# Start the first products before the shift is known, and take the RMS factors with tokens on partitions

## The chip, the cores and the metric

The kernel runs on one core of a Trainium2 chip. The metric is the device time of one execution in microseconds (us). The kernel before was run three times: median 1080.2 us, from 1079.94 to 1081.06 us. A profile of one more execution lies beside it.

Names of the engines as the profile has them: PE is TensorE (matrix products; PEld is its loading of stationary operands), DVE is VectorE, ACT is ScalarE, POOL is GpSimd, SP is SyncE, which here issues the DMAs.

## The reference, cut to what matters

Two layers of a decoder run over 512 prompt tokens and 8 sample tokens, which are kept side by side as 520 columns. Every layer begins with an RMSNorm whose result is scaled and shifted by vectors that depend on a conditioning input c (adaLN), followed by a wide projection:

```python
def rmsnorm(x, g):
    return x * lax.rsqrt(jnp.mean(x * x, axis=-1, keepdims=True) + EPS) * g
def adaln(c, w, b):
    return jnp.split((jax.nn.silu(c) @ w + b)[:, None, :], 3, axis=-1)
# even layer
shift, scale, gate = adaln(c, aw, ab)
h = rmsnorm(x, g) * (1 + scale) + shift
z = h @ w_in                      # 1024 -> 8192 features
# ... short convolution and dilated window attention on slices of z ...
x = x + gate * (out @ w_out)
# odd layer: the same wrapper, with pooling and retention;
# o of each retention head is normalised over its 256 features:
o = o * lax.rsqrt(jnp.mean(o * o, axis=-1, keepdims=True) + EPS)
```

All data are fp32, and the model width is 1024.

## The kernel before, in words

**Layout.** Features lie on the 128 partitions, tokens in the free dimension: x is eight tiles `xT[j]` of 128 x 520 (512 prompt tokens and 8 samples). An fp32 product is made of three matrix passes on operands split into a high and a low part: high data by high weight, low data by high weight, high data by low weight (`mm3`). One k step of a product (one 128-feature slice) is therefore six MATMULs, each over 256 or 264 columns; a product of eight k steps gives 128 output features for all tokens. There are 144 such weight tiles. ACT makes the high part of a weight (`w_hi`, 128 x 1024), DVE the low part (`w_lo`, two halves of 128 x 512). Lines L135 to L160 are helpers that issue the operations, so most groups of the profile carry L140 (ACT), L146, L149, L153, L154 (DVE) or L160 (PE), and a group is known by its tiles.

**Order of the work.** PE runs the products one after the other without a break. A scheduler (L181 to L215) counts one tick per k step, some 0.72 us. `at(n, f)` runs f n ticks later; `put` and `put_fill` queue attention work that is let in one piece a tick. Each engine executes its instructions in program order, so an early row that waits holds up all rows behind it on that engine. The data loads are all issued by SP.

**The beginning (L384 to L447).** x is loaded, ACT squares the tiles and DVE adds them. Four products with `on_d`, a 128 x 128 tile of 1/1024, sum over the partitions and leave the mean square of each token repeated on every partition. ACT takes the root, DVE the reciprocal (L413, L414: `r0`, 128 x 520), and POOL multiplies the eight tiles by it (L416). Then a loop over j takes the adaLN weight of one feature tile, shift and scale together (`ada_load`, `ada_mm`: eight products with 256 columns), transposes it (`ada_fin`, L348), and makes `h = x * r0 * A + S` (`h_hi`, `h_lo`). Two steps behind, k step j of the first two products runs. Head pair 0 takes its v and k from these two products and its gate and q from the next two.

**The head pairs (`head_pair`, L457 to L616).** Eight head pairs follow. Each makes four products (v, k, gate, q), then causal scores in four blocks, a softmax on DVE and ACT, transposes of the probabilities (`turn`, L543) and the sums over v (`weigh`), all let in between the k steps of the next head pair's products. DVE also works on the samples' window attention (`L573` and the 128 x 1024 products).

**The seam (L796 to L894).** The output products of layer 0 give the new x, tile by tile. A running sum of squares is multiplied by `on_d` (`ssq_add`), the root goes to ACT, two reciprocals to DVE (`r1_part`, L202 by the scheduler) and eight multiplications to POOL (`h1_scale`, L868); `h1_x` and a split then make layer 1's h. The first products of layer 1 run on x scaled but not yet normalised, and their results are multiplied by r1 (`z_first`).

**Retention (`ret_head`, L904 to L1132).** For each of four heads `norm` (L974 to L984) multiplies the head's squares by `on_d` (one product with 512 columns), takes the root on ACT (128 x 512), and DVE takes the reciprocal in two halves (`inv`, L986 to L990) ahead of `gate` (L992).

## Time and profile before

| what | value |
|---|---|
| median of three runs | 1080.2 us |
| profiled execution | 1080.08 us |
| its span | 1078.3 us |
| mean granted TensorE clock | 0.991 of full speed |
| PE busy | 1042.2 us (97%) |
| DVE busy | 638.1 us (59%) |
| ACT busy | 492.3 us (46%) |
| POOL busy | 27.4 us (3%) |

The span is the time from the first to the last instruction on the core; the profiled execution's own time is 1.8 us more. A busy time is the sum over an engine's instructions. A group's row gives the line, the engine, the operation, output and input tiles with their shapes, the count, the busy time and the mean of one in ns, then the time the engine was idle ahead of it and what ended it. A row of a timeline gives the start, the duration, the engine and the operation, and in brackets a wait ahead of it. A row of windows gives a stretch of time, its length, the busy time of PE, PEld, DVE, ACT and POOL with counts, the granted clock of PE as a share, and what the DMA did.

### The profile page before, as it was taken

The numbers are of one execution on the slowest core, as the hardware profiler recorded it, in microseconds if no ns is written. First come the engines' busy times: TensorE is split into PE (matmuls) and PEld (weight loads), VectorE is DVE, ScalarE is ACT, GpSimd is POOL, SyncE is SP. The second block draws the span as 40 slices with busy tenths as digits, with TensorE's granted clock in tenths as the row PEclk, the third lists the DMA queues.
The fourth block names the chain that finished last, engine by engine and source line by source line (L and its number), as shares of the span: only waits on it lengthen the run. The fifth ranks groups of instructions, "written<-read, shape, count | busy, mean of one in ns | idle before, by whom it ended". The sixth has DMA issues, their size and how long they took to land.

```text
span 1078.3 us, 21052 instructions
## 1 busy us (share of the span) xinstructions
PE 1042.2 (97%) x8656; PEld 989.0 (92%) x8656; DVE 638.1 (59%) x1468; ACT 492.3 (46%) x890; POOL 27.4 (3%) x45
## 2 busy tenths in 40 slices
PE   3999999999999999999999989999999999999996
PEld 1699999999989999999999989999999999999996
DVE  6556777667786444446344586565647666674443
ACT  4575667656663222223333465435454444333333
POOL 3000000000000000000000040000000000000000
PEclk9999999999999999999999999999999999999999
DMA  9486545665436355352744335272635423225212
GB/s 356 159 271 189 166 143 161 209 185 181 141 129 195 119 198 159 117 170 91 248 160 150 105 118 195 91 253 98 235 123 178 171 96 109 83 81 181 99 70 80
DMA packets 82177, 168.96 MB, mean 157 GB/s; under 512 B 7209, under 2 KB 47241, under 8 KB 79001
## 3 DMA queue, kind: packets, MB, share of 16 engines
q1 hardware_dynamic: 82080, 167.61, 46.6%
q8 instruction: 68, 1.11, 0.4%
q14 instruction: 29, 0.23, 0.1%
HBM read 149.40 MB, written 18.65 MB: 156 GB/s over the span
## 4 chain that ended last, share of the span: by engine, by line
PE 92%; DVE 4%; ACT 2%; DMA 1%; issue 1%; SPq 0%; DVEq 0%; ACTq 0%
PE mm L160 75%; PE aux L160 13%; PE aux L543 2%; DVE t L146 1%; ACT t L140 1%; DVE wlo L146 1%; DMA v<-vdr 1%; PE aux L348 0%; PE aux L1239 0%; DVE t L149 0%; DMA t<-in_x_t 0%; PE aux L463 0%; DVE t L202 0%; PE aux L918 0%; ACT whi L140 0%
## 5 line engine op out<-in xcount | busy, mean ns | idle before, releaser
L160 PE MATMUL mm<-t,whi 128*128 128x256 f32 (+1 forms) x4608 | 764.5, 287 | 7.1 <-ACT t L140 4.9
L160 PEld LDWEIGHTS mm<-t,whi 128*128 128x128 f32 x4608 | 637.3, 189 | 36.2 <-issue 21.9
L160 PE MATMUL mm<-t,wlo 128*128 128x256 f32 (+2 forms) x2304 | 465.7, 282 | 0.0
L160 PEld LDWEIGHTS mm<-t,wlo 128*128 128x128 f32 x2304 | 358.8, 189 | 0.0
L146 DVE TENSOR_TENSOR wlo<-wraw,whi 128x512 fp32r<-128x512 f32 x288 | 192.6, 699 | 52.0 <-ACT whi L140 51.7
L140 ACT ACTIVATE whi<-wraw 128x1024 fp32r<-128x1024 f32 x144 | 151.6, 1053 | 98.1 <-PE mm L160 62.9
L146 DVE TENSOR_TENSOR t<-t,t 128x520 fp32r<-128x520 f32 (+6 forms) x164 | 107.0, 652 | 96.3 <-ACT t L140 94.6
L140 ACT ACTIVATE t<-t 128x520 fp32r<-128x520 f32 (+3 forms) x116 | 70.9, 616 | 166.0 <-DVE t L149 97.8
L140 ACT ACTIVATE t<-aux 128x128 f32<-128x128 f32 (+7 forms) x148 | 67.9, 469 | 115.9 <-PE aux L160 64.8
L140 ACT ACTIVATE t<-mm 128x512 f32<-128x512 f32 (+2 forms) x116 | 56.4, 507 | 114.0 <-PE mm L160 112.5
L146 DVE TENSOR_TENSOR t<-aux,t 128x512 fp32r<-128x512 f32 (+6 forms) x120 | 60.8, 512 | 37.1 <-ACT t L140 32.0
L160 PE MATMUL aux<-t,t 64*128 64x256 f32 (+6 forms) x384 | 56.2, 329 | 0.0
L160 PE MATMUL aux<-t,v 128*128 128x512 f32 (+2 forms) x224 | 49.1, 324 | 0.6 <-DVE t L146 0.6
L521 DVE CUSTOM_DVE_ANT_0 t<-aux,t 128x128 f32<-128x128 f32 (+3 forms) x64 | 28.9, 489 | 31.9 <-PE aux L160 31.4
L160 PEld LDWEIGHTS aux<-t,t 64*128 64x128 f32 (+1 forms) x384 | 41.5, 186 | 5.4
L140 ACT ACT_TABLE_LOAD x32 | 41.1, 1283 | 1.3 <-PEq L1353 0.7
L140 ACT ACTIVATE t<-t,mn 128x128 f32<-128x128 f32 (+3 forms) x64 | 35.4, 554 | 13.3 <-DVE mn L521 13.1
L160 PEld LDWEIGHTS aux<-t,v 128*128 128x128 f32 x224 | 34.4, 188 | 1.9 <-DVE t L146 0.8
L149 DVE SCALAR_TENSOR_TENSOR big<-v,ksc,big 128x256 f32<-128x256 f32 x64 | 27.7, 480 | 10.3 <-ACT big L140 9.9
L350 DVE TENSOR_REDUCE m<-aux 128x18 f32<-128x72 f32 x24 | 5.5, 231 | 45.8 <-PE aux L348 45.8
L143 DVE COPY zs<-mm 128x8 f32<-128x8 f32 x76 | 12.1, 159 | 34.6 <-ACT t L140 33.7
L146 DVE TENSOR_TENSOR t<-mm,t 128x512 f32<-128x512 f32 (+1 forms) x24 | 16.5, 689 | 26.6 <-PE mm L160 17.4
(145 smaller groups left out, 603.2 us busy)
## 6 DMA issues: line engine op xcount, KB each, us to landing
wraw<-in_w_in_e SPq DMA_DIRECT2D x64, 512.0 KB, 6.4
wraw<-in_w_in_o SPq DMA_DIRECT2D x48, 512.0 KB, 3.2
big<-in_ada_e SPq DMA_DIRECT2D x12, 1024.0 KB, 8.3
big<-in_ada_o SPq DMA_DIRECT2D x12, 1024.0 KB, 8.5
wraw<-in_w_out_e SPq DMA_DIRECT2D x16, 512.0 KB, 3.5
big<-in_state_ret SPq DMA_DIRECT2D x16, 512.0 KB, 7.5
out_new_ret_sample<-big SPq DMA_DIRECT2D x16, 512.0 KB, 3.7
wraw<-in_w_out_o SPq DMA_DIRECT2D x16, 512.0 KB, 3.2
```

The source lines that it names most:

```text
L140: return nc.scalar.activation(out=out, in_=in_, func=func, scale=scale, **kw)
L143: return nc.vector.tensor_copy(out, in_)
L146: return nc.vector.tensor_tensor(out=out, in0=in0, in1=in1, op=op)
L149: return nc.vector.scalar_tensor_tensor(out=out, in0=in0, scalar=scalar, in1=in1, op0=op0, op1=op1)
L160: nc.tensor.matmul(out, lhsT=lhsT, rhs=rhs, start=start, stop=stop)
L350: nc.vector.tensor_reduce(out=m, in_=pt.rearrange("p s (g r) -> p s r g", g=4)[:, :, 0:9, :], op=ALU.add, axis=AX.X)
L521: nc.vector.tensor_tensor_reduce(out=sb, in0=s[:, 0:n], in1=bt[e][:, S - n:S], scale=1.0, scalar=3e38, op0=ALU.add, op1=ALU.min, accum_out=mn,
L543: nc.tensor.transpose(ep[:, c * P:(c + 1) * P], src, ident)
```

## The change

**At the beginning.** The adaLN weight is stored in another order, scale, shift and gate apart, two feature tiles to a load. The identity and the small vectors are loaded earlier. The sum of squares is taken with tokens on partitions: `rms_sums` uses a 128-token block of the squares as the stationary operand and one column of `on_d` as the moving one, so that five one-column products give a 128 x 5 tile; `rms_roots` takes its root and reciprocal, and `rms_rows` turns it into rows again by four products with the identity (128 columns each) and one of 8 columns, which ACT and DVE copy out. `x_normed` multiplies x by it on DVE instead of POOL. The first four products (v, k, gate and q of head pair 0) run on x scaled, without the shift; the first two in four rounds of two k steps, with the scale of the next two tiles made between. The shift's four adaLN groups are made inside products 3 and 4. What the shift adds to the four results is a vector per output: `shift_rows` multiplies the shift by the raw weight of each product (eight products of 128 columns, a transpose, a reduction), and `z_shift` adds it. Head pair 0's pieces come 8 ticks later (`D0`). Head pair 1 runs on x scaled too, with ten further columns that carry the shift (`z_second`). Meanwhile `h_x` and `h_split` make the full h, which head pair 2 and later use.

**At the seam.** `rms_sums`, `rms_roots` and `rms_rows` replace `ssq_add` and `r1_part`; the eight multiplications (`h1_scale`) go from POOL to DVE, one every two ticks.

**In retention.** The same three functions replace the product with 512 columns, the 128 x 512 root and the two 128 x 256 reciprocals of each head; the rows come two ticks behind the sums, and the gates at ticks 5 and 8 instead of 7 and 10.

The diff, cut to its core:

```diff
+    def rows_mm(lhs, raw):
+        n = raw.shape[2] * raw.shape[3]
+        ps = aux([P, n])
+        for k in range(KT):
+            g = 32 * (k % 4)
+            mm(ps[g:g + 32], lhs[:, k, :], raw[:, k].rearrange("p s c -> p (s c)"), k < 4, k >= 4)
...
+    def rms_sums(parts, n=T):
+        blocks = [c * P for c in range(n // P)] + ([n - P] if n % P else [])
+        pc = aux([P, len(blocks)])
+        for i, c in enumerate(blocks):
+            for k, sq in enumerate(parts):
+                mm(pc[:, i:i + 1], sq[:, c:c + P], on_d[:, 0:1], k == 0, k == len(parts) - 1)
+        return pc
+    def rms_roots(pc, scale=1.0):
+        rc = mk(cp, [P, 5], F32, "rc", 2)[:, 0:pc.shape[1]]
+        act(rc, pc, ACTF.Sqrt, bias=eps[:, 0:1], scale=scale)
+        nc.vector.reciprocal(rc, rc)
+        return rc
+    def rms_rows(rc, r):
+        pr, n = aux([P, S]), r.shape[1]
+        for i in range(4):
+            mm(pr[:, i * P:(i + 1) * P], rc[:, i:i + 1].to_broadcast([P, P]), ident, True, True)
+        act(r[:, 0:S], pr)
+        if n > S:
+            pr = aux([P, n - S])
+            mm(pr, rc[:, 4:5].to_broadcast([P, P]), ident[:, P - n + S:P], True, True)
+            vcopy(r[:, S:n], pr)
...
-    for x in xT:
-        nc.gpsimd.tensor_tensor(out=x, in0=x, in1=r0, op=ALU.mult)
...
+    rms_rows(rms_roots(rms_sums([sqa])), r0)
+    def x_normed(j):
+        vtt(xT[j], xT[j], r0, ALU.mult)
+    def x_scaled(j):
+        x, g = xT[j], mA[0][:, j, 8:9]
+        hi, lo = tr(T + 10), tr(T + 10)
+        vtt(xhs[:, j, :], x[:, S:T], mA[0][:, j, 0:NB], ALU.mult)
+        act(hi[:, 0:S], x[:, 0:S], ACTF.Copy, scale=g)
+        act(hi[:, S:T], xhs[:, j, :])
+        stt(lo[:, 0:S], x[:, 0:S], g, f(hi[:, 0:S]), ALU.mult, ALU.subtract)
+        lo_of(lo[:, S:T], xhs[:, j, :], hi[:, S:T])
+        xa.append((hi, lo))
...
+    for i in range(4):
+        for j in (2 * i, 2 * i + 1):
+            x_scaled(j)
...
+        if i < 3:
+            x_normed(2 * i + 2)
+            x_normed(2 * i + 3)
+            if i:
+                first_two(2 * i)
+            md = ada_mm(rawA[i + 1])
+            first_two(2 * i + 1 if i else 0)
+            ada_fin(0, "scale", i + 1, md)
+            if i == 0:
+                first_two(1)
+        else:
+            first_two(6)
+            first_two(7)
...
+    def z_shift(n, md):
+        m, x = zf[n]
+        ws = rows_turn(md)
+        act(x, x, ACTF.Silu if n == 2 else ACTF.Identity, bias=ws[:, 0, 8:9])
+        vtt(zs[0][:, m, :], zs[0][:, m, :], ws[:, 0, 0:NB], ALU.add)
+    for n in range(4):
+        at(1 + 2 * n, shift_rows, n)
...
+    for j in range(KT):
+        at(8 + 2 * j, h_x, j)
+        at(25 + j, h_split, j)
...
-            put(score, qb, after=Q0 + n)
+            put(score, qb, after=D0 + Q0 + n)
...
-    def h1_scale():
-        for x in xT:
-            nc.gpsimd.tensor_tensor(out=x, in0=x, in1=r1, op=ALU.mult)
+    def h1_scale(j):
+        vtt(xT[j], xT[j], r1, ALU.mult)
...
-    at(3, ssq_add, sq, False)
-    at(4, r1_part, 0)
-    at(4, r1_part, 1)
-    at(6, h1_scale)
+    at(2, r1_sums)
     for j in range(KT):
+        at(H1A - 2 + H1B * j, h1_scale, j)
         at(H1A + H1B * j, h1_x, j)
...
         def norm():
-            ms = aux([P, S])
-            mm(ms, on_d, st["sq"][0], True, True)
-            rr = tt(S)
-            act(rr, ms, ACTF.Sqrt, bias=eps[:, 0:1], scale=4.0)
+            rc = rms_roots(rms_sums(st["sq"][0:1], S), 4.0)
...
-            at(1, inv, 0)
-            at(4, inv, 1)
+            at(2, rms_rows, rc, st["rr"])
             for i in range(2):
-                at(7 + 3 * i, gate, i)
+                at(5 + 3 * i, gate, i)
```

How this moves the instructions is seen in three places. The first is PE at the start of the program. In the rows of before, `t_137` and `t_157` are the squares, `big` the adaLN weight, `mm_180` the first product.

```order
L160 MATMUL aux_159<-t_137,on_d 128x256
L160 MATMUL aux_160<-t_137,on_d 128x264
L160 MATMUL aux_159<-t_157,on_d 128x256
L160 MATMUL aux_160<-t_157,on_d 128x264
L160 MATMUL aux_182<-big_125,scT 32x256 x8
L348 MATMUL aux_195<-csm,md_191 128x128 x2
L160 MATMUL aux_207<-big_129,scT 32x256 x8
L348 MATMUL aux_226<-csm,md_216 128x128 x2
L160 MATMUL aux_240<-big_133,scT 32x256 x8
L160 MATMUL mm_180<-t_222,whi_193 128x256
```

The same place after; `rc_171` is the 128 x 5 tile, `csm` holds the identity.

```order
L160 MATMUL aux_165<-on_d,t_140 128x1 x5
L160 MATMUL aux_174<-csm,rc_171 128x128 x4
L160 MATMUL aux_180<-csm,rc_171 128x8
L160 MATMUL aux_185<-big_126,scT 32x256 x8
L354 MATMUL aux_198<-csm,md_194 128x128 x2
L160 MATMUL aux_233<-big_130,scT 32x256 x8
L160 MATMUL mm_183<-t_205,whi_219 128x256
```

The first product stands behind two adaLN groups instead of three, and the rows of r0 stand ahead of the first group.

The second place is ACT around head pair 0's last softmax block and its first transposed probabilities. In the rows of before, `t_763`, `t_765`, `t_827` and `t_829` are probabilities, `t_848` and `v_850` the turned v, `t_898` the first transposed block of probabilities, `wraw` a weight.

```order
L140 ACTIVATE whi_813<-wraw_661 128x1024
L140 ACTIVATE t_763<-t_763,ls_732 128x256
L140 ACTIVATE t_765<-t_765,ls_736 128x256
L140 ACTIVATE t_827,ls_732<-t_827,mn_731 128x512
L140 ACTIVATE t_829,ls_736<-t_829,mn_735 128x512
L140 ACTIVATE t_848<-aux_843 128x512
L140 ACTIVATE v_850<-t_848 128x8x64
L140 ACTIVATE t_827<-t_827,ls_732 128x512
L140 ACTIVATE t_829<-t_829,ls_736 128x512
L140 ACTIVATE t_898<-aux_893 128x512
```

After, the probabilities are `t_934`, `t_936`, `t_1006` and `t_1008`; rows with `mS_88,mA_86` are `h_x`, and `t_205<-t_109` is the first `h_split`.

```order
L140 ACTIVATE t_114<-t_114,mS_88,mA_86 128x512
L140 ACTIVATE t_934<-t_934,ls_891 128x256
L140 ACTIVATE t_936<-t_936,ls_895 128x256
L140 ACTIVATE t_1020<-t_969 128x512
L140 ACTIVATE t_1006,ls_891<-t_1006,mn_890 128x512
L140 ACTIVATE t_1008,ls_895<-t_1008,mn_894 128x512
L140 ACTIVATE t_115<-t_115,mS_88,mA_86 128x512
L140 ACTIVATE t_1006<-t_1006,ls_891 128x512
L140 ACTIVATE t_1008<-t_1008,ls_895 128x512
L140 ACTIVATE t_116<-t_116,mS_88,mA_86 128x512
L140 ACTIVATE t_1074<-aux_1069 128x512
L140 ACT_TABLE_LOAD
```

The rebuilding of h stands between the exponentials and the scalings, and the first transposed block (`t_1074`) stands behind both.

The third place is DVE at the seam. Before, `t_7394` is r1 and the last line's product the first one that layer 1 evicts.

```order
L146 TENSOR_TENSOR t_7373<-mS_89,t_7372 128x10
L146 TENSOR_TENSOR wlo_7429<-wraw_7153,whi_7413 128x512 x2
L202 RECIPROCAL t_7394<-t_7394 128x256
L202 RECIPROCAL t_7394<-t_7394 128x264
L149 SCALAR_TENSOR_TENSOR t_7470<-mm_7400,t_7394 128x512
```

After, r1 is `t_7524`.

```order
L146 TENSOR_TENSOR t_7503<-mS_89,t_7502 128x10
L395 RECIPROCAL rc_7562<-rc_7562 128x5
L146 TENSOR_TENSOR wlo_7571<-wraw_7287,whi_7543 128x512
L143 COPY t_7524<-aux_7579 128x8
L146 TENSOR_TENSOR wlo_7571<-wraw_7287,whi_7543 128x512
L149 SCALAR_TENSOR_TENSOR t_7609<-mm_7530,t_7524 128x512
L143 COPY ws_7610<-mm_7530 128x9
L146 TENSOR_TENSOR zs_95<-mm_7530,t_7524 128x8
L146 TENSOR_TENSOR zs_95<-zs_95,ws_7610 128x8
L146 TENSOR_TENSOR t_6328<-t_6328,t_7524 128x520
```

The two long reciprocals are replaced by one of 128 x 5, and the multiplications by r1 join DVE's queue.

## The prediction

> **What bounds the kernel now.** I read the page first, then the waits of PE, then windows and timelines of the three places that the change touches.

> ```profile
> span 1078.3 us, 21052 instructions
> PE 1042.2 (97%) x8656; PEld 989.0 (92%) x8656; DVE 638.1 (59%) x1468; ACT 492.3 (46%) x890; POOL 27.4 (3%) x45
> ```

> PE is busy for 97% of the span: what the change can give lies in the beginning and in PE's few waits, and a matrix pass added anywhere else is paid in full. The waits (engine, place, what was waited for: us in total, times, longest):

> ```profile
> PE aux L160 <- DVE t L146: 12.7, 4, 10.7
> PE mm L160 <- ACT t L140: 4.9, 2, 4.4
> PE aux L911 <- ACT t L140: 3.7, 1, 3.7
> PE aux L918 <- ACT t L140: 1.3, 2, 1.0
> ```

> 10.7 of the first row is the start, up to the first sum of squares; the second row holds the first product's wait for its data; L911 and L918 are the seam. The stretches (length, busy of PE, PEld, DVE, ACT, POOL, then the granted clock):

> ```profile
> 20.00:25.00 5.00, 1.07 (x16) 0.50 (x16) 4.96 (x6) 0.81 (x1) 5.00 (x5) 0.71 1.01 415
> 25.00:30.00 5.00, 2.74 (x11) 2.44 (x12) 4.96 (x6) 2.67 (x4) 4.45 (x4) 0.50 0.35 146
> 76.00:82.00 6.00, 6.00 (x54) 6.00 (x53) 5.01 (x12) 5.55 (x12) 0.00 (x0) 1.00 0.51 154
> 82.00:88.00 6.00, 6.00 (x59) 5.24 (x58) 6.00 (x9) 3.45 (x8) 0.00 (x0) 1.00 0.06 24
> 625.00:630.00 5.00, 3.39 (x28) 3.17 (x26) 4.36 (x6) 1.73 (x3) 5.00 (x5) 1.00 0.32 108
> 634.00:636.00 2.00, 2.00 (x11) 2.00 (x11) 1.75 (x5) 1.97 (x4) 0.00 (x0) 0.50 0.00 0
> ```

> At 20 to 30 us PE is half idle or more while DVE and POOL are full, and its clock is halved. At 76 to 88, head pair 0's softmax, PE has no gap, but ACT, then DVE, has hardly a moment free: this is where the change puts more work on both. The last two rows are the seam: a wait, and half the clock behind it.

> **The beginning.** Rows of the timeline of before, DVE then PE (start, us, operation):

> ```profile
> 6.66 3.92 DVE L146 TENSOR_TENSOR t<-t,t 128x520 f32<-128x520 f32 x5 [0.41 <-ACT t L140]
> 10.72 3.81 PE L160 MATMUL aux<-t,on_d 128*128 128x256 f32 x8 [10.72 <-DVE t L146]
> 14.46 1.44 PE L160 MATMUL aux<-big,scT 128*32 128x256 f32 x16
> 28.06 0.80 PE L160 MATMUL mm<-t,whi 128*128 128x256 f32 x2 [1.56 <-DVE t L146]
> 63.60 0.63 PE L160 MATMUL mm<-t,whi 128*128 128x256 f32 x4
> 84.75 1.07 PE L160 MATMUL aux<-big,scT 128*32 128x256 f32 x16
> 85.75 0.51 PE L160 MATMUL mm<-t,whi 128*128 128x256 f32 x2
> ```

> Product 1 gets going at 28.06, product 5 (the first of head pair 1) starts at 63.60. An adaLN group of 256 columns costs PE 85.75 − 84.75 = 1.00.

> What small products cost is read where they stand inside a product. Here four calls with 4 columns (two passes each), and elsewhere one with 512, are let in:

> ```profile
> 396.88 0.40 PE L160 MATMUL mm<-t,wlo 128*128 128x256 f32 x2
> 397.12 0.95 PE L160 MATMUL aux<-csm,t 128*128 128x4 f32 x8
> 397.93 0.73 PE L160 MATMUL mm<-t,whi 128*128 128x256 f32 x4
> 398.50 0.40 PE L160 MATMUL mm<-t,wlo 128*128 128x256 f32 x2
> ...
> 399.22 0.40 PE L160 MATMUL mm<-t,wlo 128*128 128x256 f32 x2
> ...
> 682.95 0.40 PE L160 MATMUL mm<-t,wlo 128*128 128x256 f32 x2
> 683.18 1.02 PE L160 MATMUL aux<-t,on_d 128*128 128x512 f32 x2
> ...
> 684.52 0.40 PE L160 MATMUL mm<-t,wlo 128*128 128x256 f32 x2
> ```

> Undisturbed, one wlo row follows the other in 399.22 − 398.50 = 0.72, a k step; eight make a product, 5.75. With the small calls between it is 1.62, with the large one 1.57: 0.90 for four small calls, 0.225 each, and 0.85 for 512 columns, so 0.21 for a call of 128.

> The new chain. DVE's six sums end at 10.58; the seventh, now needed too, makes 11.3. Five one-column calls at half clock 2.2, root, reciprocal of 128 x 5 and their handing over 0.8, five row calls at half clock 2.1: r0 is there at about 16.4. The adaLN group (1.44 as above) ends at 17.5 or a little later; its copy, transposes, reduction and two scales take some 2.0, and then ACT has two scaled tiles and a weight ahead of the first product: 0.8 + 0.8 + 1.0. So it starts at about 22.0. From there to product 5 PE has 8 x 1.44 (two products), 3 x 1.25 (scale groups with transposes), 11.5 (products 3 and 4) and 4 x 1.25 (shift groups), 31.75 in all. It waits besides: after the transposes of the second and third round stands only the product that needs them, and reduction, scales, ACT's scaled tile and DVE's part of it take 2.2; in the first round one product step of 1.44 covers most of that. With 2.2 + 2.2 + 0.8, product 5 starts at 59.0: **−4.6**. The bounds are −6.5 (a start at 21.0 and chains of 1.7) and −2.5 (1.7 lost to half the clock, as at 20 to 30 us, and 0.4 more for the sums).

> POOL's leaving is in this already. The same DVE operations took, at 17.6 to 29.2 us (POOL busy) and at 30 to 47 us (POOL idle):

> ```profile
> L146 DVE TENSOR_TENSOR wlo<-wraw,whi 128x512 fp32r<-128x512 f32 x3 | 4.2, 1411 | 0.0
> L154 DVE TENSOR_SCALAR mA<-m,bsc,pv 128x9 f32<-128x9 f32 x2 | 2.7, 1327 | 0.0
> ```

> ```profile
> L146 DVE TENSOR_TENSOR wlo<-wraw,whi 128x512 fp32r<-128x512 f32 x3 | 2.0, 680 | 0.0
> ...
> L154 DVE TENSOR_SCALAR mA<-m,bsc,pv 128x9 f32<-128x9 f32 x5 | 1.4, 285 | 0.0
> ```

> I use the lower values, since POOL is idle there. [...]

> **What the shift costs PE later.** Four groups of shift rows: eight calls of 128 columns each. From 1.00 at 256 columns, half is 0.50; I take 0.58 because of the price of small calls (ends 0.50 and 1.00). Four: 2.3. Four transposes at 0.12: 0.5. Ten more columns on four products: 0.4. The turn of head pair 0's v, which stood before 63.60, now stands behind: 0.4. Together **+3.6**, with no wait beside it to hide in.

> **Head pair 1's products: a queue on ACT, then on DVE.** Rows for the durations, then one of DVE's window work, then PE's first transpose of head pair 0's probabilities:

> ```profile
> L140 ACT ACTIVATE t<-t,mS,mA 128x512 f32<-128x512 f32 x8 | 6.5, 808 | 3.0 <-DVE mA L154 3.0
> L140 ACT ACT_TABLE_LOAD x32 | 41.1, 1283 | 1.3 <-PEq L1353 0.7
> L140 ACT ACTIVATE whi<-wraw 128x1024 fp32r<-128x1024 f32 x144 | 151.6, 1053 | 98.1 <-PE mm L160 62.9
> L146 DVE TENSOR_TENSOR t<-t,t 128x520 fp32r<-128x520 f32 x64 | 44.7, 698 | 33.1 <-ACT t L140 32.9
> ```

> ```profile
> 81.52 1.21 DVE L573 TENSOR_REDUCE t<-big 128x16 f32<-128x1024 f32 x1
> ```

> ```profile
> 79.09 0.60 PE L543 MATMUL aux<-csm,t 128*128 128x128 f32 x4
> ```

> Before, the first transpose came 79.09 − 63.60 = 15.5 after product 5's start. Now it stands 8 ticks later (5.7), behind the shift rows with their transposes (2.8) and v's turn (0.4): 24.4. ACT's rows from there to the scaling that this transpose reads stand in a fixed order: two table loads 2.6, seven rebuilt tiles at 0.71 (neighbouring rows overlap by 0.1) 5.0, three weights 2.9, and by the same rule from their mean durations eight exponentials 4.2, four scalings 1.7, and 8.4 for evictions, biases, splits and small rows: 24.8. At two places ACT must wait for a product's end or a maximum, 1.9 at least; then one scaling more. So the scaling is ready at some 27.4 and PE waits 3.0.

> Behind it DVE. From the first rebuilt tile's low part to the last one's it has 8 of these (0.6 each), six low parts of transposed blocks, a window product, two reductions (1.1 each) and two halves of a weight, 12.6 in all; PE's nine ticks, six turns and an adaLN group come to 10.1. Before, DVE was already full there (82 to 88) and PE did not wait. Transposes that DVE has not read hold PSUM buffers, and PE waits for those. The excess is 2.5; its bounds are 0 (buffers take it) and 4.8 (all eight low parts are extra). Together **+5.5**, bounds 0 and 9.5, the latter with half the clock behind a longer gap (1.7, as at the seam).

> [...]

> **The seam.**

> ```profile
> 632.06 0.66 PE L911 MATMUL aux<-csm,t 128*128 128x128 f32 x4 [3.67 <-ACT t L140]
> ```

> ```profile
> L868 POOL TENSOR_TENSOR t<-t,t 128x520 f32<-128x520 f32 x8 | 12.1, 1548 | 17.7 <-DVE t L202 17.7
> L202 DVE RECIPROCAL t<-t 128x256 f32<-128x256 f32 x1 | 1.7, 1746 | 0.0
> ```

> PE gets ten one-column calls (2.25) and five of rows (1.1) and is rid of two sums of 520 columns (0.87 each): +1.6. It waits about 0.45 for the last square. The 3.67 goes, since two reciprocals (3.4) leave DVE's queue ahead of the evicted v and their neighbours are no longer slowed by POOL; so does the half clock behind it (3.4 us at half speed, 1.7), and L918's 1.3 falls to about 0.7. DVE gets eight multiplications of 0.6, one in two ticks, which fit. Together 1.6 + 0.45 − 3.67 − 1.7 − 0.6 = **−3.9**; bounds −5.5 and 0 (the multiplications take the place of the reciprocals, and PE waits nearly as before).

> **Retention.** Per head +0.90 (four small calls) +0.87 (rows) −0.85 (512 columns) = 0.92; four heads **+3.7**. What ACT and DVE save there buys nothing: no wait of PE in that part stands in the list above. Bounds 2.0 and 4.5.

> **The sum** against the profiled execution's 1080.08 (span 1078.3; the median, 1080.2, lies 0.1 above it): −4.6 + 3.6 + 5.5 − 3.9 + 3.7 = +4.3, **1084.4 us**. A difference of 0.2%, 2.2 us, is about what a measurement of this kernel can tell from none.

> **The rivals.** *No queue.* ACT and DVE catch up before PE needs them. For it: before, PE did not wait at 76 to 88. Against it: 24.8 us of ACT rows in a fixed order. Sum −1.2: 1078.9.

> *No queue, and a beginning at its best.* PE starts at 21.0 and the chains of the rounds take 1.2 instead of 2.2: −7.6 in place of −4.6, sum −4.2, 1075.9. For it: DVE without POOL's company is idle for much of each round. Against it: the chain crosses three engines, and nothing stands behind it on PE that could go first. This is the other side; it decides from the point where head pair 0's scaling is done before PE has run 24.4 us past product 5's start.

> *A long queue.* All eight low parts count and a gap passes the length that halved the clock: 3.0 + 4.8 + 1.7 in place of 5.5, sum +8.3, 1088.4. For it: DVE's 6.00 of 6.00 at 82 to 88. Against it: at 76 to 82 PE ran on although ACT was busy for 5.55 of 6.

> **How the numbers follow.** Forecast 0.46, no queue 0.20, no queue with the best beginning 0.24, long queue 0.10. Faster takes the third and 0.04 of the second; same takes 0.16 of the second and 0.04 of the forecast's low end; slower the rest: 0.28, 0.20, 0.52. The range goes from 0.9 below the third case (the seam's better bound) to 1.1 above the fourth: 1075.0 to 1089.5. The forecast's own range is 1082 to 1087.

> **What would show it.** Product 5 near 59.0; a wait of PE near 83 for ACT's scaling, and waits of PE on DVE's low parts just behind; no 3.67 wait at the seam and a full clock there; a k step with four one-column calls 0.9 longer. It is wrong if PE runs through head pair 1 without a wait, or if a wait of the beginning stays that I have taken as gone.

## The result, and the profile after

The change makes the kernel slower: 1100.42 us (median of four runs, 1099.19 to 1101.0) against 1080.18 us, a ratio of 1.0183 with a 95% interval of 1.017 to 1.0196. The forecast was 1084.4 us in a range of 1075.0 to 1089.5: the direction was right, the size a fifth of what came.

The profiled execution of the changed kernel took 1101.0 us. Its page and the waits of PE:

```profile
span 1099.2 us, 21418 instructions
PE 1059.0 (96%) x8814; PEld 1007.5 (92%) x8814; DVE 625.9 (57%) x1518; ACT 503.7 (46%) x928; POOL 4.2 (0%) x31
```

```profile
PE aux L160 <- DVE t L146: 18.0, 7, 12.9
PE mm L160 <- ACT t L140: 2.8, 2, 1.4
PE mm L160 <- ACT whi L140: 2.5, 1, 2.5
PE aux L669 <- ACT t L140: 2.2, 1, 2.2
PE aux L1065 <- ACT t L140: 2.1, 2, 1.1
PE aux L160 <- issue: 1.3, 1, 1.3
```

The seam's wait of 3.7 (L911 before) is gone from the list, as forecast. New are L669, the transposes of head pair 0's probabilities waiting for ACT, and five more us in the first row. But the listed waits grow far less than the span does (20.9 us): PE's busy time is 16.8 us higher. A busy PE can be a PE at half clock (4.00 of 4.00 us busy at a clock of 0.50 from 632 to 636 us, below), so I read from the starts of the products where the time came in. A product has 48 MATMULs on `mm` tiles; counting them in PE's timeline gives the start of each (us):

| start of product | before | after | later by | in this stretch |
|---|---|---|---|---|
| 1 | 25.70 | 24.19 | −1.50 | |
| 5 (head pair 1) | 63.60 | 64.84 | 1.24 | beginning: +1.24 |
| 13 (head pair 3) | 130.43 | 146.04 | 15.61 | head pairs 1 and 2: +14.37 |
| 81 (first of layer 1) | 610.67 | 626.72 | 16.05 | +0.44 |
| 89 (first of the second retention head) | 680.79 | 698.05 | 17.25 | seam: +1.20 |
| start of the last MATMUL | 1068.59 | 1089.50 | 20.91 | retention and the rest: +3.66 |

One of the two old sums of the seam, 0.9, stood ahead of product 81 (at 601.16 us before), so that part of the seam's change lies in the row above it: taken whole, the seam lost some 0.3. Product 5 also varies with the execution: in the four other profiles below whose start is that of the kernel before and not filled, it begins between 63.54 and 65.30, and in the four others whose start is that of the change (in one with wider sums), between 64.94 and 65.57. The loss at the beginning is therefore about 1 us, and the gain that was forecast is not there.

The windows of the changed kernel, with the granted clock as the third number from the end, show half a clock in four places: twice in the beginning (from 26.18 and 43.24 us, for 3.41 each), behind the wait of head pair 1 (from 94.44, for 3.41), and at the seam.

```profile
24.00:28.00 4.00, 3.59 (x19) 3.19 (x20) 3.83 (x7) 1.36 (x3) 0.00 (x0) 0.77 0.88 367
40.00:44.00 4.00, 2.31 (x14) 1.86 (x14) 2.76 (x10) 1.65 (x4) 0.00 (x0) 0.91 0.92 341
44.00:48.00 4.00, 3.87 (x22) 3.67 (x21) 0.17 (x1) 1.13 (x3) 0.00 (x0) 0.67 0.12 48
92.00:96.00 4.00, 1.82 (x11) 1.58 (x9) 2.30 (x6) 4.00 (x9) 0.00 (x0) 0.81 0.99 363
96.00:100.00 4.00, 4.00 (x28) 4.00 (x28) 1.27 (x3) 3.97 (x6) 0.00 (x0) 0.77 0.90 250
104.00:108.00 4.00, 2.63 (x18) 2.34 (x17) 4.00 (x7) 1.83 (x4) 0.00 (x0) 1.00 0.25 57
628.00:632.00 4.00, 3.80 (x27) 3.71 (x27) 1.29 (x5) 3.19 (x6) 0.00 (x0) 0.79 0.21 78
632.00:636.00 4.00, 4.00 (x21) 4.00 (x20) 0.28 (x1) 0.21 (x1) 0.00 (x0) 0.50 0.00 0
```

The last row is the one to learn from: PE is busy for 4.00 of 4.00 us, nobody waits, and it has 21 MATMULs at a clock of 0.50, where `seam_only` (below) has 36 in the same place at 1.00. The record of the granted clock has the seam's half clock from 630.34 us for 6.83 us.

PE's timeline of the changed kernel at the places that the prediction named:

```profile
12.91 2.27 PE L160 MATMUL aux<-on_d,t 128*128 128x1 f32 x10 [12.91 <-DVE t L146]
24.19 0.75 PE L160 MATMUL mm<-t,whi 128*128 128x256 f32 x4 [2.54 <-ACT whi L140]
42.22 0.51 PE L160 MATMUL mm<-t,whi 128*128 128x256 f32 x2 [1.40 <-ACT t L140]
43.01 0.62 PE L160 MATMUL mm<-t,whi 128*128 128x256 f32 x2 [0.28 <-DVE t L149]
67.06 0.64 PE L160 MATMUL aux<-v,t 128*32 128x128 f32 x16 [1.32 <-issue]
94.59 0.48 PE L669 MATMUL aux<-csm,t 128*128 128x128 f32 x1 [2.18 <-ACT t L140]
104.89 0.69 PE L160 MATMUL aux<-t,v 128*128 128x512 f32 x2 [0.85 <-DVE t L146]
109.41 0.39 PE L160 MATMUL aux<-t,v 128*128 128x256 f32 x1 [1.92 <-DVE t L146]
628.67 2.51 PE L160 MATMUL aux<-on_d,t 128*128 128x1 f32 x18 [0.20 <-ACT t L140]
```

And ACT just ahead of 94.59, in its order: a tile of h is rebuilt (`t<-t,mS,mA`) between the exponentials and the scaling for which PE waits.

```profile
92.42 0.71 ACT L140 ACTIVATE t<-t,mn 128x512 f32<-128x512 f32 x1
93.03 0.19 ACT L140 ACTIVATION_READ_ACCUMULATOR t<-t,mn 128x1 f32 x1
93.12 0.80 ACT L140 ACTIVATE t<-t,mS,mA 128x512 f32<-128x512 f32 x1
93.83 1.32 ACT L140 ACTIVATE t<-t,ls 128x512 f32<-128x512 f32 x2
```

### The profile page after: what moved, and what is told of

Its sections match the earlier page's. It is cut to its first block, busy times and chain, and to the rows that moved or that the text cites. A ratio compares the mean times of both kernels' runs of the same rounds, so it can differ in the third digit from the quotient of the medians.

```text
span 1099.2 us, 21418 instructions
## 1 busy us (share of the span) xinstructions
PE 1059.0 (96%) x8814; PEld 1007.5 (92%) x8814; DVE 625.9 (57%) x1518; ACT 503.7 (46%) x928; POOL 4.2 (0%) x31
## 4 chain that ended last, share of the span: by engine, by line
PE 88%; ACT 4%; DVE 4%; DMA 1%; issue 1%; SPq 0%; DVEq 0%; ACTq 0%
PE mm L160 72%; PE aux L160 14%; ACT t L140 3%; DVE t L146 2%; PE aux L669 1%; DMA v<-vdr 1%; ACT whi L140 1%; DVE t L149 1%; PE aux L354 1%; DVE wlo L146 0%; DMA t<-in_x_t 0%; PE aux L1377 0%; SPq L157 0%; ACT L140 0%; DVE t L699 0%
## 5 line engine op out<-in xcount | busy, mean ns | idle before, releaser
L160 PE MATMUL mm<-t,whi 128*128 128x256 f32 (+2 forms) x4608 | 766.5, 288 | 6.0 <-ACT t L140 2.8
L160 PEld LDWEIGHTS mm<-t,whi 128*128 128x128 f32 x4608 | 639.1, 190 | 33.5 <-issue 21.4
L160 PE MATMUL mm<-t,wlo 128*128 128x256 f32 (+2 forms) x2304 | 468.7, 284 | 0.2 <-DVE wlo L146 0.2
L160 PEld LDWEIGHTS mm<-t,wlo 128*128 128x128 f32 x2304 | 360.9, 189 | 0.6 <-DVE wlo L146 0.6
L146 DVE TENSOR_TENSOR wlo<-wraw,whi 128x512 fp32r<-128x512 f32 x280 | 182.9, 685 | 43.5 <-ACT whi L140 43.1
L140 ACT ACTIVATE whi<-wraw 128x1024 fp32r<-128x1024 f32 x140 | 147.4, 1053 | 98.1 <-PE mm L160 63.6
L146 DVE TENSOR_TENSOR t<-t,t 128x520 fp32r<-128x520 f32 (+7 forms) x189 | 119.1, 636 | 99.3 <-ACT t L140 97.6
L140 ACT ACTIVATE t<-t 128x520 fp32r<-128x520 f32 (+4 forms) x126 | 73.8, 591 | 156.3 <-DVE t L149 96.0
L140 ACT ACTIVATE t<-aux 128x512 f32<-128x512 f32 (+7 forms) x154 | 71.4, 473 | 119.7 <-PE aux L160 74.2
L140 ACT ACTIVATE t<-mm 128x512 f32<-128x512 f32 (+2 forms) x112 | 54.0, 504 | 108.1 <-PE mm L160 103.9
L146 DVE TENSOR_TENSOR t<-aux,t 128x512 fp32r<-128x512 f32 (+6 forms) x120 | 61.0, 514 | 36.6 <-ACT t L140 31.5
L160 PE MATMUL aux<-t,t 64*128 64x256 f32 (+6 forms) x384 | 56.6, 329 | 0.3 <-DVE t L146 0.3
L160 PE MATMUL aux<-t,v 128*128 128x512 f32 (+2 forms) x224 | 49.5, 325 | 3.4 <-DVE t L146 3.4
L160 PEld LDWEIGHTS aux<-t,t 64*128 64x128 f32 (+1 forms) x384 | 41.8, 186 | 6.1 <-DVE t L146 0.6
L140 ACT ACT_TABLE_LOAD x32 | 41.1, 1283 | 1.3 <-PEq L1489 0.7
L140 ACT ACTIVATE t<-t,mn 128x128 f32<-128x128 f32 (+3 forms) x64 | 35.4, 554 | 11.8 <-DVE mn L647 11.5
L160 PEld LDWEIGHTS aux<-t,v 128*128 128x128 f32 x224 | 34.5, 188 | 5.1 <-DVE t L146 3.0
L356 DVE TENSOR_REDUCE m<-aux 128x18 f32<-128x72 f32 (+1 forms) x28 | 6.4, 227 | 47.8 <-PE aux L354 47.8
L143 DVE COPY zs<-mm 128x8 f32<-128x8 f32 x72 | 11.7, 162 | 38.1 <-ACT t L140 32.9
L146 DVE TENSOR_TENSOR t<-mm,t 128x512 f32<-128x512 f32 (+1 forms) x24 | 16.6, 690 | 26.7 <-PE mm L160 17.8
```

The lines of the kernel that those rows point to most:

```text
L140: return nc.scalar.activation(out=out, in_=in_, func=func, scale=scale, **kw)
L143: return nc.vector.tensor_copy(out, in_)
L146: return nc.vector.tensor_tensor(out=out, in0=in0, in1=in1, op=op)
L160: nc.tensor.matmul(out, lhsT=lhsT, rhs=rhs, start=start, stop=stop)
L356: nc.vector.tensor_reduce(out=m, in_=pt.rearrange("p s (g r) -> p s r g", g=4)[:, :, 0:9, :], op=ALU.add, axis=AX.X)
```

## The experiments

**One part at a time.** The first question is whether the parts add, or hinder one another.

`seam_only` is the kernel before with the seam of the change:

```diff
-    at(3, ssq_add, sq, False)
-    at(4, r1_part, 0)
-    at(4, r1_part, 1)
-    at(6, h1_scale)
+    at(2, r1_sums)
     for j in range(KT):
+        at(H1A - 2 + H1B * j, h1_scale, j)
         at(H1A + H1B * j, h1_x, j)
```

> The kernel before with the seam of the change alone. Theory A (each part costs what the two traces show at its place): the products behind the seam start 1.2 us later than before, 1081.4 us, with the clock halved for some 6.8 us between the sums and the first products of layer 1, and no 3.67 us wait. Theory B (the seam by itself gains what was forecast, and what was lost there came from the state in which the new beginning left the queues): about 3.9 us faster, 1076.3 us, with the clock not halved.

Measured: 1078.57 us against 1080.77, ratio 0.998 (0.9971 to 0.9989). Neither theory: the seam alone is 2.2 us faster. In its profile the products behind the seam (product 89) stand 2.79 us earlier relative to product 5 than before, and its clock is full where the changed kernel had half:

```profile
612.00:616.00 4.00, 3.81 (x34) 3.72 (x33) 1.54 (x4) 2.89 (x6) 0.00 (x0) 1.00 0.18 70
616.00:620.00 4.00, 4.00 (x36) 4.00 (x35) 0.77 (x2) 0.60 (x1) 0.00 (x0) 1.00 0.23 68
```

So the same instructions gained in one kernel and lost in the other, and the clock is what differs. All profiles with the new seam bear this out. From product 81 to 89, the kernel before takes 70.12 us; the new seam takes 68.19 to 68.28 in the six profiles with a full clock there, 69.79 in the one with half a clock for 3.41 us, and 71.33 and 71.34 in the two with half a clock for 6.83.

`ret_only` is the kernel before with the change's retention norm (`rms_sums`, `rms_roots`, `rms_rows` and the gates two ticks earlier).

> The kernel before with the change's retention norm alone. Theory A (small calls on a full engine are paid in full): four times 0.9 us more, 1083.7 us, and each head's products 0.9 us later. Rival (the calls hide in gaps between passes, and the shorter reciprocals let something start earlier): within 0.5 us of before, 1080.2 us.

Measured: 1084.48 us against 1080.77, +3.7, ratio 1.0036 (1.0023 to 1.0049); the last product ends 3.75 us later. The price per call was read rightly. In its timeline one wlo row follows the next by 1.60 where four one-column calls stand between and by 1.61 where the rows stand, against 0.72 undisturbed:

```profile
682.93 0.40 PE L160 MATMUL mm<-t,wlo 128*128 128x256 f32 x2
683.16 0.95 PE L160 MATMUL aux<-on_d,t 128*128 128x1 f32 x8
683.97 0.72 PE L160 MATMUL mm<-t,whi 128*128 128x256 f32 x4
684.53 0.40 PE L160 MATMUL mm<-t,wlo 128*128 128x256 f32 x2
684.78 0.65 PE L160 MATMUL mm<-t,whi 128*128 128x256 f32 x4
685.26 0.41 PE L160 MATMUL mm<-t,wlo 128*128 128x256 f32 x2
685.50 1.05 PE L160 MATMUL aux<-csm,rc 128*128 128x128 f32 x8
686.31 0.72 PE L160 MATMUL mm<-t,whi 128*128 128x256 f32 x4
686.87 0.40 PE L160 MATMUL mm<-t,wlo 128*128 128x256 f32 x2
```

`begin_only` is the changed kernel with the seam and the retention norm of before.

> The change with the seam and retention of before, so the beginning and the delayed head pair 0 alone. Theory A (the parts add): 1.2 us at product 5, 14.4 us more up to product 13, and nothing later: 1095.8 to 1096.5 us. Rival (the beginning costs less by itself and the parts hinder one another): under 1092 us.

Measured: 1097.41 us against 1080.77, ratio 1.0153 (1.0139 to 1.0167); product 5 is 1.73 us later than before, product 13 16.11. The beginning costs some 16.6 us by itself, a little above theory A; the rival falls. So: beginning and head pairs +16.6, retention +3.7, seam −2.2, together 18.1 where the whole change has 20.2. The difference of 2.1 is less than the 3.1 that the seam's half clock costs.

**The clock.** `seam_wide` is `seam_only` with wider sums:

```diff
-        pc = aux([P, len(blocks)])
+        pc = aux([P, len(blocks), 64])
...
-                mm(pc[:, i:i + 1], sq[:, c:c + P], on_d[:, 0:1], k == 0, k == len(parts) - 1)
-        return pc
+                mm(pc[:, i, :], sq[:, c:c + P], on_d[:, 0:64], k == 0, k == len(parts) - 1)
+        return pc[:, :, 0]
```

> The same seam, but each sum over tokens streams 64 columns of ones instead of one; the result is read from the first column. The calls take about the same time, since each is bound by loading 128 x 128 of squares. Theory A1 (the clock is granted by what the array streams, and ten one-column calls in a row count as idle although the engine shows as busy): the clock is not halved, about 3.4 us less than the one-column version, 1078.0 us. Theory A2 (the clock is halved by the short wait ahead of the calls or by where the window falls): halved as with one column, the same time within 0.5 us, 1081.4 us.

Measured: 1079.01 us against 1080.77, ratio 0.9985 (0.9976 to 0.9994), the clock full at the seam. Since `seam_only` was not halved either, this told nothing apart by itself. `clock_cols` asks the question without the seam: bursts of calls that nobody reads, among the output products of layer 0.

```diff
+    def burst(n, cols):
+        ps = aux([P, cols])
+        for _ in range(n):
+            mm(ps, ident, on_d[:, 0:cols], True, True)
...
     for m in range(KT):
         ps = mm2()
+        if m in (2, 4):
+            burst(40, 1 if m == 2 else 128)
```

> The kernel before with two bursts of products that nobody reads among the output products of layer 0: 40 calls with one column ahead of output tile 2, 40 calls with 128 columns ahead of tile 4; each burst is some 8.5 to 9 us, PE counting as busy throughout. Theory A1 (the clock follows the columns streamed): the granted clock is halved during and just behind the first burst, and stays full in the second; about 1080 + 17.5 + 3 = 1101 us. Theory A2 (the clock follows whether PE has instructions): full in both, 1097.5 us.

Measured: 1106.17 us (one run). The two bursts in PE's timeline, and a window within and behind each:

```profile
538.21 14.54 PE L160 MATMUL aux<-on_d,csm 128*128 128x1 f32 x80
...
580.94 9.10 PE L160 MATMUL aux<-on_d,csm 128*128 128x128 f32 x80
```

```profile
544.00:548.00 4.00, 4.00 (x21) 4.00 (x20) 0.78 (x2) 0.61 (x2) 0.00 (x0) 0.50 0.39 131
584.00:588.00 4.00, 4.00 (x39) 4.00 (x38) 2.26 (x6) 1.79 (x4) 0.00 (x0) 1.00 0.65 177
```

40 calls of one column took 14.54 us, 40 calls of 128 columns 9.10. The total is 5 us above theory A1's figure, which had 8.5 to 9 us for each burst and did not reckon that the one-column calls would themselves be slower at half clock (14.54 us). The record of the granted clock has half a clock from 540.98 us for 17.07 us, in and behind the first burst, and none at the second. PE was busy for 4.00 of 4.00 us in both windows, so whether PE has instructions did not decide: the clock was 0.50 at the calls of one column and 1.00 at those of 128. Theory A1 holds here.

> The change with each of its sums over tokens streaming 64 columns of ones instead of one, at the beginning, at the seam and in retention. Theory A1 (a burst of one-column calls counts as idle for the clock, and whether it halves depends on where the free-running window cuts it): no halving at the seam in the profile and none in the other runs, the seam 2 to 3 us faster than before instead of 1.2 slower, 1097.4 us, beginning and head pairs as in the change. Theory A2 (the halving at the seam has another cause): halved as in the change, 1100.4 us.

Measured: 1098.66 us (1098.37 to 1098.84, five runs) against 1080.95 on that chip, ratio 1.0163 (1.0149 to 1.0176). The seam (product 81 to 89) is 1.93 us shorter than before instead of 1.20 longer, with a full clock in the profile, although the first call came 0.92 us into the window:

```profile
628.00:632.00 4.00, 3.85 (x34) 3.71 (x33) 1.57 (x6) 3.19 (x6) 0.00 (x0) 1.00 0.33 125
632.00:636.00 4.00, 4.00 (x36) 4.00 (x35) 1.48 (x4) 0.60 (x1) 0.00 (x0) 1.00 0.01 1
```

The size fits A1 at the seam (3.1 us). The median is 1.3 us above the expected 1097.4; in this profile product 5 was 0.7 us later than in the change's, which is a part of it, and the rest stays open.

**Head pairs 1 and 2.** `no_rebuild` leaves out a part of the computation: the shift is missing in h from head pair 2 on.

```diff
     for j in range(KT):
-        at(8 + 2 * j, h_x, j)
-        at(25 + j, h_split, j)
+        pass
```

> The change without the rebuilding of h (no h_x, no h_split): head pairs 2 to 7 and the convolution run on x scaled without the shift, so this part of the computation is left out. Theory Q (a queue: the eight rebuilt tiles and their splits stand in ACT's and DVE's order ahead of what PE needs): the 2.2 us wait for ACT's scaling near 92 us, the half clock behind it (1.7) and the waits for DVE at 102 to 110 us (about 3.3) go, 7.2 us less than the change, 1093.2 us (1091 to 1095). Rival D (the delayed pieces of head pair 0 collide with those of head pair 1, whoever rebuilds): 1098 us or more, with the waits in place.

Measured: 1093.04 us against 1080.42, ratio 1.0118 (1.0103 to 1.0134). Product 13 is 10.36 us later than before instead of 15.61: the rebuilding costs 5.3 us there, not 7.2. (The seam's clock, which was full in this profile, gave 3.1 more.) The waits shrink but do not go:

```profile
92.89 0.33 PE L668 MATMUL aux<-csm,t 128*128 128x128 f32 x1 [0.43 <-ACT t L140]
98.13 0.44 PE L668 MATMUL aux<-csm,t 128*128 128x128 f32 x2 [0.87 <-DVE t L146]
104.84 0.38 PE L160 MATMUL aux<-t,v 128*128 128x256 f32 x1 [0.76 <-DVE t L146]
```

Theory Q has the larger part, and rival D a smaller one: even without the rebuilding head pair 0's pieces, 8 ticks late, wait for ACT and DVE. `later` moves the rebuilding:

```diff
-        at(8 + 2 * j, h_x, j)
-        at(25 + j, h_split, j)
+        at(22 + j, h_x, j)
+        at(30 + j, h_split, j)
```

> The change with the rebuilding moved: h_x at ticks 22 to 29 instead of every second tick from 8 to 22, h_split at ticks 30 to 37 instead of 25 to 32. Theory Q (it is the place in the order that costs): ACT reaches the first scaling some 4 us earlier, the splits no longer stand among the low parts of the transposed blocks, 1093 to 1096 us. Rival W (the amount of work costs, wherever it stands): 1099 us or more, with the waits moved by a few us.

Measured: 1100.87 us against 1080.42, ratio 1.0196 (1.0179 to 1.0214); product 13 at +15.69. The wait for the scaling falls to 0.39 and no half clock follows it, but PE then waits elsewhere, for tiles of h itself:

```profile
99.00 0.44 PE L669 MATMUL aux<-csm,t 128*128 128x128 f32 x2 [1.71 <-DVE t L146]
...
106.63 0.50 PE L160 MATMUL mm<-t,whi 128*128 128x256 f32 x2 [1.29 <-DVE t L146]
110.44 0.51 PE L160 MATMUL mm<-t,whi 128*128 128x256 f32 x2 [0.70 <-ACT t L140]
```

Theory Q, as far as it blamed the place in the order, falls; rival W holds for this move. At both places that were tried, ACT and DVE have more to do than the time of these products leaves: from product 5 to 13 it is 81.2 us in the change and 81.1 in `later`.

**The beginning.** `begin_fill` puts products that nobody reads where PE waits (`pe_fill(n, cols)`: n calls of on_d with a weight):

```diff
             md = ada_mm(rawA[i + 1])
+            if i == 0:
+                pe_fill(2)
             first_two(2 * i + 1 if i else 0)
             ada_fin(0, "scale", i + 1, md)
             if i == 0:
                 first_two(1)
+            else:
+                pe_fill(1)
+                pe_fill(1, 256)
```

> The change with products that nobody reads, put on PE where it waits in the first rounds: two of 512 columns behind the second scale group, one of 512 and one of 256 columns behind the transposes of the third and fourth group, each shorter than the wait that it fills. Theory G (the clock is halved after a window in which PE streamed for less than about half the time, so the waits cost more than their length): the two halved windows near 26 and 43 us go, product 5 starts 3.4 us earlier, 1097.0 us. Rival (the halving does not follow from these waits, or the filling delays what it stands ahead of): 1100 us or more.

Measured: 1097.65 us against 1080.42, ratio 1.0159 (1.0143 to 1.0174). The clock is full from 21.64 us to the last output products (1.00 from 24 to 32 and from 40 to 48, mean 0.998), so the halving in the beginning does follow from the waits: all five profiles with the change's beginning unfilled have a halved window in the rounds (between 36 and 47 us), and the two with it filled have none. But product 5 starts only 0.91 us earlier than in the change, not 3.4. Products 1 and 2 run interleaved; in the second half of their MATMULs (35.70 to 47.56, now 36.25 to 46.64) 1.5 us are won; the first half, 24.19 to 35.70 and now 24.76 to 36.25, gives nothing, since PE waited there for ACT and DVE in any case, and product 1 itself comes 0.57 later.

The same profile shows what the half clock of head pair 1 cost. There is none here, yet product 5 to 13 takes 81.2 us, as in the change. PE gets to its next transposes sooner and waits for DVE instead:

```profile
93.71 0.33 PE L679 MATMUL aux<-csm,t 128*128 128x128 f32 x1 [2.17 <-ACT t L140]
99.46 0.41 PE L679 MATMUL aux<-csm,t 128*128 128x128 f32 x2 [1.34 <-DVE t L146]
```

The half clock therefore cost nothing in that place: ACT and DVE set the pace.

`fill_x_first` adds that the identity and the small vectors are loaded behind x:

```diff
-    load(csm[:, 0:P], a["c_small"][:, 0:P])
     xT = [tt() for _ in range(KT)]
     for j in range(KT):
         load(xT[j], a["x_t"][:, j, :])
-        if j == 1:
-            load(pv, a["small_t"])
+    load(csm[:, 0:P], a["c_small"][:, 0:P])
+    load(pv, a["small_t"])
```

> The filled beginning (begin_fill) with the identity and the small vectors loaded behind the eight tiles of x, not ahead of and among them, and the small additions that read them taken behind the sum of squares. Theory L (the two loads hold back x, and the sum of squares with it): PE's first sums start near 11.6 us instead of 12.9, product 1 and product 5 each 1.3 us earlier than in begin_fill, 1096.3 us. Rival (the weights of the scale, loaded behind, decide): product 1 within 0.3 us of begin_fill, 1097.6 us.

Measured: the first sums start at 11.35 us, product 1 at 23.73 (1.03 earlier than in `begin_fill`), product 5 at 62.26 (1.67 earlier): theory L. The time, 1098.03 us against 1080.48 (ratio 1.0158, 1.0143 to 1.0174), is none the less no lower. The seam was halved for 6.83 us in this profile and not in that of `begin_fill`, and the runs differ in the same way: two of the four of `begin_fill` have a mean clock of 0.998 and took 1097.02 and 1097.13, the other two, at 0.994 and 0.995, 1098.16 and 1098.95; all four of `fill_x_first`, at 0.994 and 0.995, took 1097.16 to 1098.44.

**A version that beats both.** `before_fill` puts 24, 4 and 16 such calls of 128 columns into PE's waits at the start of the kernel before:

```diff
+    pe_warm(24)
     ssq, r0 = [aux([P, 512]) for _ in range(2)], tt()
...
             md = ada_mm(raw0[j])
+        if j == 2:
+            pe_warm(16)
...
             ada_fin(0, "ss", j, md)
+        if j == 1:
+            pe_warm(4)
```

> The kernel before with products that nobody reads on PE where it waits at the start: 24 of 128 columns ahead of the sums of squares, 4 behind the second transposes, 16 behind the third adaLN group. Theory G (the clock follows the columns streamed, so filling keeps it up): the sums run at full clock (1.9 us instead of 3.8) and the halved 10 us from 22 on shrink; 2 to 4 us less than before, 1077.4 us. Rival (the chain over DVE and POOL sets the start of product 1 anyway): at most the 1.9 us of the sums, and less where the loads decide, 1079 us or more.

Measured: 1080.4 us against 1080.48, ratio 0.9996 (0.9987 to 1.0005): nothing that can be told from none. The sums do run in 2.02 us instead of 3.81, but product 1 starts at 26.60: the two long reciprocals, POOL's multiplications and DVE's rows slowed beside them (1.25 us for a 128 x 8 multiplication at 21.00, 0.15 for the same at 28.85) stand between, as the rival had it. In this profile, product 5 does start 2.1 us earlier (61.54), but its execution is the fastest of the eleven (1078.66), and with the same filling in `best` product 5 starts at 63.71, so that gain is not a steady one.

`best` joins that filling with `seam_wide`.

> The kernel before with that filling and with the change's seam, its sums streaming 64 columns. If the two add: 2.2 us for the seam (as the seam alone measured) and what the filling gives: 1075.2 us. If the filling gives nothing: 1078.5 us.

Measured: 1078.84 us against 1080.48, ratio 0.9982 (0.9973 to 0.9991). It is the seam alone once more. The three versions with that seam alone, or with the filling, are 1.6 to 2.2 us faster than the kernel before; `seam_only`, at 0.998 (0.9971 to 0.9989), is the simplest of them.

## Why the prediction was right or wrong

The sum was −4.6 + 3.6 + 5.5 − 3.9 + 3.7; measured were +1.24 for the first term, +14.37 for the next two together, +1.20 (0.3 with the old sum ahead of product 81) and +3.66. Three steps failed: the chain and the rounds of the beginning were too short (5.8 us), the waits and the added work of head pairs 1 and 2 too small (5.3 us), and the reading of the clock, which left out the half clock at the seam (3.1 us). Two of the five terms had the wrong sign; that the direction came out right is due to the head pairs and retention alone.

**The beginning, wrong.** "It starts at about 22.0": it started at 24.19. The sums began at 12.91 instead of 11.3, because two loads stand ahead of and among the tiles of x; moving them made it 11.35 (`fill_x_first`). My sum has no term for the loads: I had not looked at what the new order on SP's queue puts ahead of x. The rest of this term's miss is in the rounds: from product 1 to product 5 I had 37.0 us and it took 40.65. The second halved window cost 1.5 of that (`begin_fill`); the first cost nothing. Products 3 and 4 with the shift groups took 17.28 (47.56 to 64.84) where I had 16.5. What is left, about 1.4, I only place in the first rounds, where four halves of two weights and two normalised tiles stand in DVE's order ahead of the next scale; that was not tried by itself.

**The clock, wrong.** For head pair 1 and the seam I tied half a clock to a wait of the seam's length, 3.67: none behind the 3.0 of my sum in head pair 1, one in the long queue, none where the seam's wait was gone. That step failed in most places, and no run shows a length of wait from which the clock is halved. In the change it was halved behind a wait of 2.18 (at 94.44 us), behind two of 1.40 and 0.28 (at 43.24), and behind one of 0.20 at the seam (at 630.34). In the 3.41 us ahead of these, PE was at work for 1.38, 1.72 and 3.22 us; the last, with 17 one-column MATMULs, had the same effect as the two that were partly idle. The trace of before already spoke against my reading. In the two windows of 3.41 us ahead of its half clocks, PE was at work for 1.19 and 1.00 us; the second lies only in part in the wait of 3.67, to which I had put the half clock down:

```profile
18.66:22.07 3.41, 1.19 (x18) 0.50 (x16) 3.41 (x4) 0.81 (x1) 3.41 (x4) 1.00 0.98 399
629.65:633.06 3.41, 1.00 (x9) 1.00 (x10) 2.83 (x9) 2.38 (x4) 2.07 (x2) 1.00 0.00 0
```

**Head pair 1, the mechanism right, the sizes too small.** I had a wait of 3.0 for ACT's scaling: 2.18 came, at the instruction that I named, though later than I had it: PE got there 27.6 us after product 5's start instead of 24.4, and the scaling was ready at 29.7 instead of 27.4. I had 2.5 for DVE: 0.24, 0.85, 1.92 and 0.30 are 3.3, at the places behind it. Not in my sum was the 1.32 ahead of the first shift rows, where the list names no releaser. In `begin_fill` the same wait, 1.37, ends with DVE's copy of the shift (L143), which stands in DVE's order behind two halves of a weight and a copy for the samples. The 1.7 for half the clock that one of my rivals added is not a cost here, as `begin_fill` shows. It is simplest to count there, at full clock: of the 14.4 us from product 5 to 13, waits are 8.2 where I had 5.5, and PE is busy for 6.2 more where I had 3.6. The MATMULs that were added are those that I listed; the other 2.6 stay open (the modelled ends of MATMULs may cover short waits). `no_rebuild` shows that 5.3 us of the whole come from the rebuilding of h, and `later` that they do not go away by moving it; the remaining 9 come from the delay and the shift together, which were not taken apart.

**The seam, right by itself and wrong in the whole.** The 3.67 wait went, L918's 1.3 did not fall to 0.7 but is 2.1 (L1065 now), and alone the seam gains 2.2 us against the 3.9 forecast. In the changed kernel's profile it lost 1.2 from product 81 to 89, because the ten one-column calls brought the clock down for 6.83 us, which costs 3.1: what I had priced at 0.225 a call had a second price in the change and in `fill_x_first`, and none in `seam_only`.

**Retention, right.** 0.92 a head were forecast, 0.9 measured; four heads 3.7 forecast, 3.66 in the change and 3.7 alone.

Of the rivals the long queue, 1088.4, came nearest, by its longer waits and not by its half clock there; no case let the beginning lose. All my cases took its gain as certain in sign, and that narrowed the range. (The range's lower end is also misreckoned: the seam's better bound lies 1.6 below the third case, not 0.9. It did not bear on the result.)

## What to carry to other kernels

On an engine that is busy for 97% of the span, an operation that moves work there from idle engines is paid call by call: in `ret_only` four calls of one column cost 0.88 us and four of 128 columns 0.89. When the order of a start is changed, follow the load queue too, not only the compute engines. Put the granted clock beside busy time in every window: the 6.83 us of half clock at the seam, with PE busy for 4.00 of 4.00 us, were 3.1 us of lost time that no list of waits shows, while the 3.41 us in head pair 1 cost nothing, because PE would have waited for another engine behind it (81.2 us from product 5 to 13 with the half clock and without).

## What the runs showed of the hardware

In `clock_cols`, forty fp32 calls with 128 columns took 9.10 us and forty with one column 14.54 us; at the latter the clock was halved (from 540.98 us for 17.07 us) although PE had no gap (4.00 of 4.00 us busy from 544 to 548). With 64 columns instead of one in the seam's ten calls the clock was full in three profiles, at 0.92 (`after_wide`), 0.96 and 3.24 us into the window.

The columns can be counted for every such window. I took all windows of the 3.41 us grid in the profiles before and after that begin at full clock and hold only MATMULs on the whole 128 x 128 array, 457 in all, and the columns of the MATMULs that start in each, those of the fp32 calls (sums, transposes, rows) twice. Seven were followed by half a clock: two behind the last product, with no MATMUL, and five with 2340, 2632, 2684, 2856 and 2856 columns. Of the others one has 2856, and the rest 4240 or more. A window full of product rows would have some 7400 (an estimate from six MATMULs of 256 or 264 columns in a k step of 0.72). The change has both outcomes at one count: it was halved behind the window with waits of 1.40 and 0.28 (39.83 to 43.24 us), and not behind the one with waits of 1.41 and 0.29 two windows earlier (33.01 to 36.42), both with 2856 columns. For windows with calls on a part of the array, as the adaLN groups are, this count does not hold: before, a window with 16 such MATMULs, 4096 columns, was halved (18.66 to 22.07 us, then 0.50), and in the change one with 16 and two transposes, 4608 columns, was not (19.35 to 22.77).
